# A two-layer fp32 trunk on one core: seven block products for eight in the output projections' second halves, and two hand-written orders changed

## The chip, the core and the metric

The kernel runs on one core of a Trainium2 chip. The core has a matrix engine (TensorE, PE in the profile), whose weight loads are listed apart as PEld, and four others: VectorE (DVE), ScalarE (ACT), GpSimd (POOL) and SyncE (SP). Here SP and POOL issue transfers and compute nearly nothing. The metric is device time in microseconds (us) of one execution; lower is better. A difference of about 0.2% (4.3 us here) is what a measurement of this kernel can tell from no change.

## The reference

The input is 256 tokens by 2048 features in fp32. Layer 0 is a recurrent mixer, layer 1 a windowed attention, and each ends in an output projection and is followed by a squared-ReLU MLP:

```
proj  = rms_norm(h) @ w_in                       # layer 0
lru   = rg_lru(conv(x_lru), gates) * gelu(y_lru)  # 1024 columns
hg    = hgrn2(q, f, v, g)                         # 8 heads, 1024 columns
h     = h + concat(lru, hg) @ w_out               # 2048 x 2048
h     = h + square(relu(rms_norm(h) @ w1)) @ w2   # 2048 x 8192 x 2048

q,k,v = split(rms_norm(h) @ w_qkv)                # layer 1, 16 heads of 128
o     = dilated causal attention(q, k, v)
h     = h + o @ w_o                               # 2048 x 2048
h     = h + square(relu(rms_norm(h) @ w1)) @ w2
out   = rms_norm(h)
```

The change touches `@ w_out` and `@ w_o`, the order of work in the gates of `rg_lru`, and the order in which the first block of each MLP takes its weights.

## The kernel before, in words

**Precision.** Each fp32 operand of a large product is split in two parts: `hi`, a copy rounded to the matrix engine's fp32r type, and `lo`, the rest. A product takes three matmuls: hi by hi, hi by lo, lo by hi. For a tile of weights (128 x 2048, 1 MB) ScalarE makes `hi` (line 116, "cast") and VectorE makes `lo` by a subtraction (line 117, "split").

**Weights.** The list `units` holds every tile in the order of use. `unit()` takes the next and calls `fetch()`, which loads the tile two places ahead (SP queue), casts it and splits it. Raw tiles, `hi` and `lo` have three buffers each, so the cast of a tile waits until the matmuls of the tile three places before it are done.

**Output projections.** `out_project` (line 655) runs over four column groups n of 512 columns. `tokens` (line 335) makes one group: four weight tiles (`kgs`, each with four blocks of 128 rows), two token halves j, three matmuls each: 96 matmuls of 512 columns. With `by_k` the matmuls run over the row blocks i outside and over j inside, otherwise the other way round; the first group of both projections has `by_k`. The two sums (`ps`) go into PSUM banks named `p`, three of them in turn, and `add_res` adds them to the residual `xres`. `to_features` queues the transposes to the feature layout; `turn_some` lets them run between weight tiles.

**Seven products for eight.** Both MLP products and the values of layer 1 take column groups in pairs, in `blocks` (line 663). Over half of the rows the 2x2 blocks (token halves by column groups) are multiplied with seven products instead of eight, by Winograd's form of Strassen's scheme: units `a`, `t1`, `t2`, `c`, `t3`, `d`, `t4`, 12 matmuls each. The other half of the rows is done plainly by four units `n` of 24 matmuls. The seven need sums of weight tiles (made in `combine` by a VectorE addition, line 148, and by accumulating transfers that POOL issues, into tiles `s` and `t`), sums of the left operand (`formx` or `formh`, made by `combos` and `part_forms`), and row blocks in the order `PAIRED`. `ORDERS` gives the order of the 11 units. `second` (line 780) is the pair for `@ w2`, which adds its results to `xres`.

**Order.** A planner orders the instructions of each engine by priorities (`stream` for casts, `urgent` for evictions) and by a timeline of its own. Orders by hand are added as dependencies: `mm` chains the matmuls of the large products, `after` puts one instruction behind another, `lut` keeps ScalarE's table functions together. In `lru_gates` (line 549) the weight tile fetched at that point is loaded at once, but its cast is put behind the fourth of the eight gate sigmoids (`late`, `behind`, `gates[3:4]`). The product of the last attention head, `po` (lines 932 and 933), is not in the chain, and the planner places it.

**Names.** In the traces a name is that of the tile: `p<-hi,bufb` is a large product of the left operand in `bufb` with `hi`; `po`, `pd`, `pt`, `pl` are other PSUM banks; `xall` is the residual; `z`, `q`, `gr`, `gi`, `xc` are tiles of the recurrent group.

Of the kernel before, what the change touches and what calls it, by code (L numbers as in the profile page):

```python
# [10 lines left out]
F32 = mybir.dt.float32  # L11
# [5 lines left out]
OP = mybir.AluOpType  # L17
# [3 lines left out]
P = 128  # L21
S = 256
D = 2048
KB = D // P
# [17 lines left out]
def trunk_kernel(ctx, tc, head, x, xtok, cols, tab, masks, pos, fin, w_in, w_gate, w_out, w_qkv, w_o, w1, w2, out):  # L42
# [27 lines left out]
    units = []  # L70
# [3 lines left out]
    def plan(src, n):  # L74
        units.extend((src, i) for i in range(n))

    order_of = lambda src, i: ORDERS[0 if src is w1 else 2 if src is w2 and i == 120 else 1]

    def plan2(src, i):
        for what, u in order_of(src, i):  # L80
# [4 lines left out]
    for step in ORDER.split():  # L85
        src, first, n = where[step[0]]
        units.extend((src, first(int(step[1])) + i) for i in range(n))
    units.extend((w_out, 4 * n + g) for n in range(4) for g in (2, 3, 0, 1))
    for layer in range(2):
        if layer:  # L90
            for v, heads in ((0, 24), (32, 8)):
                plan2(w_qkv, v)
                units.extend((w_qkv, v + 8 + i) for i in range(heads))
            plan(w_o, 16)
        for q in range(4):
            for src in (w1, w2):
                for n in range(0, 4, 2):
                    plan2(src, layer * 64 + q * 16 + 4 * n)
    at = [0, 0]

    class Weights:
        def __init__(self, raw, step=2048, behind=()):
# [3 lines left out]
            self.behind = list(behind)  # L106
            for at in range(0, 2048, step) if step else ():
                self.split(at, step)

        def split(self, at, n, w=None):  # L110
            h, l = self.part(at, n)
            if w is None:
                w = self.raw[:, at:at + n]
            else:
                h, l = (t.rearrange("p (k c) -> p k c", c=512) for t in (h, l))
            casts[:] = [after(A.copy(h, w), self.behind)]  # L116
            i = V.tensor_tensor(l, w, h.bitcast(F32), OP.subtract)  # L117
# [5 lines left out]
    def fetch(late=None):  # L123
        u = at[0]
        if u >= len(units):
            return
        at[0] += 1
        src, i = units[u][:2]
        with stream():
            if len(units[u]) > 2:  # L130
                combine(u, *units[u])
                return
            r = wraw.tile([P, 2048], F32, name="raw")
            loads[:] = [after(nc.sync.dma_start(r, src[i]), [])]
            if late is not None:
                late.append((u, r))
                return
            made[u] = Weights(r, 1024)

    held, waiting, read = {}, [], []  # L140
# [1 line left out]
    def combine(u, src, i, what, i0):  # L142
        def load(name, j, home=wraw):
            held[name] = home.tile([P, 2048], F32, name="raw" if home is wraw else name)
            nc.sync.dma_start(held[name], src[j])

        def add(to, x, y):
            return V.tensor_tensor(held[to], held[x], held[y], OP.add)
# [12 lines left out]
        if ahead == ("t2",):  # L161
            load("c", i0 + 5)
            nc.gpsimd.dma_start(held["t1"], src[i0 + 5], accum_op=OP.add)
            if src is w2 and i0 == LATE_SUM:
                make()
                after(add("s", "s", "c"), [made[u].ins.name])
                return
            add("s", "s", "c")
        make(2048 if what != "t2" else 0)
        if what == "t2":  # L170
            waiting.append(made[u])
        if what == "c":
            nc.gpsimd.dma_start(held["s"], src[i0 + 1], accum_op=OP.add)
# [25 lines left out]
    def unit(src, i, late=None):  # L199
        u = at[1]  # L200
        assert units[u][0] is src and units[u][1] in (None, i), (u, i)
        at[1] += 1
        if u + 2 >= at[0]:
            fetch(late)
        return made.pop(u)

    chain = []
# [1 line left out]
    def mm(*args, **kw):  # L209
        chain[:] = [after(T.matmul(*args, **kw), chain)]  # L210
# [121 lines left out]
            V.scalar_tensor_tensor(t, t, -0.5, v, op0=OP.mult, op1=OP.mult)  # L332
            V.scalar_tensor_tensor(r, t, 1.5, r, op0=OP.add, op1=OP.mult)

    def tokens(src, i0, mov, kgs=(0, 1, 2, 3), by_k=False):
        ks = range(KB)
        ps = [pmm.tile([P, 512], F32, name="p") for _ in range(2)]
        for g in kgs:
            w = unit(src, i0 + g)
            order = [(j, i) for i in range(4) for j in range(2)] if by_k else \  # L340
                [(j, i) for j in range(2) for i in range(4)]
            for j, i in order:
                k = ks[4 * g + i]
                h, l = w.part(i * 512, 512)
                xh = mov[:, k, j * P:j * P + P]
                xl = mov[:, k, S + j * P:S + j * P + P]
                first, last = g == kgs[0] and i == 0, g == kgs[-1] and i == 3
                mm(ps[j], xh, h, start=first, stop=False)
                mm(ps[j], xh, l, start=False, stop=False)
                mm(ps[j], xl, h, start=False, stop=last)  # L350
            turn_some(1)
        return ps

    def tokens_group(src, i0, rt=None, by_k=False, kgs=(0, 1, 2, 3), behind=()):
# [192 lines left out]
        split_to(bufb[:, b], xc[:, b])  # L547

    def lru_gates(gp):
        late, gates = [], []  # L550
        w = unit(w_gate, gp, late)
        gr = wk.tile([P, 4, S], F32, name="gr", bufs=1)
        gi = wk.tile([P, 4, S], F32, name="gi", bufs=1)
        for m in range(4):
            b = 4 * gp + m
            for gate, (g, bname) in enumerate(((gr, "b_a"), (gi, "b_i"))):
                p = pmm.tile([P, 512], F32, name="p")
                direct(p, w, [(gate * 8 + 2 * m + k, bufb[:, (b // 2) * 2 + k], k == 0, k == 1)
                              for k in range(2)])
# [102 lines left out]
    nrm = out_project(w_out, "nmlp0", (2, 3, 0, 1))  # L662
# [117 lines left out]
    def second(i0, n0, nrm, r2, r2n, done, gains):  # L780
        def to_x(bank, j, n, r, last):
            at = slice(n * 512, n * 512 + 512)
            with urgent():
                read[:] = [after(V.scalar_tensor_tensor(xres[:, j, at], bank, r[:, j:j + 1], xres[:, j, at],
                                                        op0=OP.mult, op1=OP.add), [])]
                if nrm and last:
                    nrm.add(j, n, 0, S if ending and (j, n) == (1, LAST) else 512)
# [19 lines left out]
        def u3(bank):  # L807
            to_x(bank, 1, n0 + 1, r2n, True)
            done(n0 + 1)

        blocks(w2, i0, n0, bufb, formh,
               {"a": lambda b: to_x(b, 0, n0, r2, False), "t1": lambda b: to_x(b, 1, n0 + 1, r2, False),
                "t2": u2, "t3": u3, **ends},
               lambda n, j, b: to_x(b, j, n0 + n, r2, (n, j) != (1, 1)))
# [2 lines left out]
    def mlp(layer, nrm, nxt, gname):  # L817
# [34 lines left out]
                second(layer * 64 + q * 16, n, ends, r2, r2n, done, gains if ends and not gname and not n else None)  # L852
        return fing

    nx1 = Norm()
    mlp(0, nrm, nx1, "nmix1")
    pairs.close()
# [71 lines left out]
    def mix(hd, st, vg, bank="po", bufs=1):  # L929
        vs = slice((hd % 8) * P, (hd % 8) * P + P)  # L930
        po = psc.tile([P, S], F32, name=bank, bufs=bufs)
        T.matmul(po, vg[:, 0, vs], st[:, :S], start=True, stop=False, skip_group_check=True)  # L932
# [6 lines left out]
    lastv = []  # L939

    def values(i0):
        v = vgs.tile([P, 2, 2, 512], F32, name="vg")
# [131 lines left out]
def _layout(a):  # L1074
# [25 lines left out]
    def gate(w):  # L1100
# [42 lines left out]
```

## Time and profile before

| | |
|---|---|
| time, median of 3 runs | 2151.3 us (2151.23 to 2152.33) |
| time of the profiled execution | 2151.35 us |
| its span, first to last instruction | 2149.5 us |
| granted clock of TensorE | 0.999 |
| HBM read | 481.76 MB, 225 GB/s over the span |
| layer 0's output projection | about 332.4 to 423.6 us of the span |
| layer 1's output projection | about 1379 to 1472.5 us of the span |

The profile page gives busy time and share of each engine, the chain of work that ended last, and groups of instructions by line. The view of waits names for each engine what ended its idle time. The view of windows gives busy time of each engine in a stretch; after the two times come the length, then PE, PEld, DVE, ACT and POOL busy with counts, the granted clock, the DMA share and GB/s. The timeline lists instructions with start and duration in us; a row that ends in x2 merges two, and brackets hold the idle time before it and its releaser.

### The profile page before, as it was taken

Reading aid. Unit: us, or ns where it says so; the run is one execution under the profiler, and the core shown is the slowest. Engines: PE = TensorE matmul, PEld = TensorE weight load, DVE = VectorE, ACT = ScalarE, POOL = GpSimd, SP = SyncE. Lnnn points to the kernel's source line nnn. Section 1 sums busy time; section 2 is a strip of 40 time slices with the busy share of each in tenths; the row PEclk is TensorE's granted clock in tenths of the full one; section 3 lists DMA queues with packets and bytes.
Section 4 is the critical chain, followed back from the end, with each engine's and each line's share of the span. In section 5 each row is a group of like instructions: output and inputs, shape, how many; then the busy total and the mean of one; then the engine's idle time right before and its main releaser. Section 6 shows DMA issues by size and latency. Waiting matters only on the chain.

```text
span 2149.5 us, 27705 instructions
## 1 busy us (share of the span) xinstructions
PE 2136.2 (99%) x11018; PEld 1830.3 (85%) x11018; DVE 1786.9 (83%) x2087; ACT 1267.6 (59%) x1407; POOL 61.8 (3%) x77
## 2 busy tenths in 40 slices
PE   9999999999999999999999999999999999999998
PEld 8999998888888888888888888888888888888887
DVE  7776787788888888889988897867988988888897
ACT  7444485566466566557665545456655755755764
POOL 0000000000000000000000000000000000000000
PEclk9999999999999999999999999999999999999999
DMA  8544445588878888887785556457878788787885
GB/s 323 175 157 157 154 149 209 179 240 268 249 240 263 257 243 243 277 245 234 240 268 198 173 160 232 157 185 226 237 240 283 240 240 260 262 241 243 272 261 156
DMA packets 68160, 485.64 MB, mean 226 GB/s; under 512 B 7600, under 2 KB 7856, under 8 KB 10048
## 3 DMA queue, kind: packets, MB, share of 16 engines
q1 hardware_dynamic: 57600, 410.89, 52.0%
q0 software_dynamic: 10144, 72.39, 18.3%
q8 instruction: 86, 1.41, 0.3%
q10 hardware_dynamic: 288, 0.61, 0.1%
q14 instruction: 42, 0.34, 0.0%
HBM read 481.76 MB, written 2.10 MB: 225 GB/s over the span
## 4 chain that ended last, share of the span: by engine, by line
PE 96%; ACT 2%; DVE 1%; DMA 0%; issue 0%; SPq 0%
PE p L210 66%; PE pd L210 13%; PE po L210 12%; PE pl L213 2%; PE pl L489 1%; PE pt L210 1%; DVE lo L117 1%; ACT hi L116 1%; DMA both_in<-in_head 0%; PE pl L911 0%; ACT gi L241 0%; ACT L241 0%; PE po L932 0%; PE pd L924 0%; ACT gr L241 0%; DVE xc L577 0%
## 5 line engine op out<-in xcount | busy, mean ns | idle before, releaser
L116 ACT CAST hi<-raw 128x2048 fp32r<-128x2048 f32 (+1 forms) x462 | 679.1, 1494 | 564.2 <-PE p L210 343.0
L117 DVE TENSOR_TENSOR lo<-raw,hi 128x2048 fp32r<-128x2048 f32 (+1 forms) x462 | 810.9, 1771 | 206.2 <-ACT hi L116 190.9
L210 PE MATMUL p<-hi,bufb 128*128 128x512 f32 x1408 | 449.0, 391 | 1.5 <-DVE z L438 1.1
L210 PE MATMUL p<-bufa,hi 128*128 128x256 f32 (+1 forms) x1792 | 367.2, 317 | 0.1
L210 PE MATMUL p<-hi,bufa 128*128 128x512 f32 x1136 | 363.3, 390 | 0.7 <-ACT bufa L271 0.7
L210 PEld LDWEIGHTS p<-hi,bufb 128*128 128x128 f32 x1408 | 264.3, 188 | 56.8 <-DVE z L438 1.5
L210 PEld LDWEIGHTS p<-bufa,hi 128*128 128x128 f32 x1792 | 294.9, 190 | 18.6 <-DVE hz L438 0.3
L210 PE MATMUL p<-lo,bufb 128*128 128x512 f32 x704 | 274.2, 390 | 0.0
L210 PE MATMUL p<-bufa,lo 128*128 128x256 f32 x1152 | 256.2, 287 | 0.0
L210 PEld LDWEIGHTS p<-hi,bufa 128*128 128x128 f32 x1136 | 213.1, 188 | 45.0 <-ACT bufa L271 0.9
L117 DVE TENSOR_TENSOR lo<-s,hi 128x2048 fp32r<-128x2048 f32 x102 | 233.1, 2285 | 14.5 <-ACT hi L116 12.3
L116 ACT CAST hi<-s 128x2048 fp32r<-128x2048 f32 x102 | 195.1, 1913 | 51.7 <-PE po L210 22.2
L210 PE MATMUL p<-lo,bufa 128*128 128x512 f32 x568 | 221.4, 390 | 0.2 <-DVE lo L117 0.2
L210 PEld LDWEIGHTS p<-bufa,lo 128*128 128x128 f32 x1152 | 189.7, 191 | 2.7
L210 PEld LDWEIGHTS p<-lo,bufb 128*128 128x128 f32 x704 | 132.2, 188 | 26.9
L210 PEld LDWEIGHTS p<-lo,bufa 128*128 128x128 f32 x568 | 106.6, 188 | 22.6 <-DVE lo L117 0.6
L210 PE MATMUL pd<-hi,bufa 128*128 128x512 f32 x288 | 95.2, 392 | 0.0
L210 PE MATMUL p<-hi,formx 128*128 128x512 f32 x288 | 94.8, 390 | 0.0
L117 DVE TENSOR_TENSOR lo<-t,hi 128x2048 fp32r<-128x2048 f32 x34 | 77.8, 2288 | 13.0 <-ACT hi L116 13.0
L210 PE MATMUL po<-hi,bufa 128*128 128x512 f32 x256 | 84.9, 393 | 0.0
L210 PE MATMUL p<-hi,formh 128*128 128x512 f32 x256 | 84.0, 389 | 0.0
L210 PE MATMUL pd<-hi,bufb 128*128 128x512 f32 x256 | 83.0, 389 | 0.0
(307 smaller groups left out, 2892.0 us busy)
## 6 DMA issues: line engine op xcount, KB each, us to landing
raw<-in_w SPq DMA_DIRECT2D x224, 1024.0 KB, 6.5
raw<-in_w_qkv SPq DMA_DIRECT2D x46, 1024.0 KB, 4.9
raw<-in_w_in SPq DMA_DIRECT2D x45, 1024.0 KB, 4.9
t<-in_w SPq DMA_DIRECT2D x32, 1024.0 KB, 6.4
t<-in_w POOLq DMA_DIRECT2D x32, 1024.0 KB, 8.9
s<-in_w POOLq DMA_DIRECT2D x32, 1024.0 KB, 9.3
raw<-in_w_out SPq DMA_DIRECT2D x16, 1024.0 KB, 4.9
raw<-in_w_o SPq DMA_DIRECT2D x16, 1024.0 KB, 4.8
```

What stands on the lines that cost most here:

```text
L116: casts[:] = [after(A.copy(h, w), self.behind)]
L117: i = V.tensor_tensor(l, w, h.bitcast(F32), OP.subtract)
L210: chain[:] = [after(T.matmul(*args, **kw), chain)]
L213: chain[:] = [after(T.transpose(out_, in_, ident), chain)]
L489: T.matmul(pl[:, j], kq[:, js], halves(qp[:, js], c, True), start=True, stop=True)
```

## The change

1. **Both output projections.** Column groups 0 and 1 go through `tokens` as before. Groups 2 and 3 go through `second`, as one pair of seven products for eight, with both multipliers 1.0 and -1.0. The weights come in the order `PAIRED`, so each `kgs` tile of the first 1024 rows holds blocks 0, 2, 4, 6 or 1, 3, 5, 7. `mixed_forms` makes the sums of the left operand out of `bufb` for each of four pairs of row blocks, at the places that `then` gives. In layer 0 the first group no longer has `by_k`.
2. **The first block of each MLP** takes its units in the order `ORDERS[1]` (n7 before n6) and no longer `ORDERS[0]`, and the first block of layer 1's MLP makes one sum of weights behind a split instead of ahead of it.
3. **The gates.** The order that put a cast behind the gate sigmoids is gone: the tile is cast where it is fetched.
4. **The last head.** Its two products are put into the matmul chain ahead of the second of the four row blocks of the last weight tile of layer 1's first column group.

```diff
-    order_of = lambda src, i: ORDERS[0 if src is w1 else 2 if src is w2 and i == 120 else 1]
+    order_of = lambda src, i: ORDERS[0 if src is w1 and i not in (0, 64, ) else 2 if src is w2 and i == 120 else 1]
...
-    units.extend((w_out, 4 * n + g) for n in range(4) for g in (2, 3, 0, 1))
+    units.extend((w_out, 4 * n + g) for n in range(2) for g in (2, 3, 0, 1))
+    plan2(w_out, 8)
...
-            plan(w_o, 16)
+            plan(w_o, 8)
+            plan2(w_o, 8)
...
-            casts[:] = [after(A.copy(h, w), self.behind)]
+            casts[:] = [after(A.copy(h, w), [])]
...
-            if src is w2 and i0 == LATE_SUM:
+            if (src is w2 and i0 == LATE_SUM) or (src is w1 and i0 == 64):
...
-    def tokens(src, i0, mov, kgs=(0, 1, 2, 3), by_k=False):
-        ks = range(KB)
+    def tokens(src, i0, mov, kgs=(0, 1, 2, 3), by_k=False, behind=(), then=()):
+        ks = PAIRED if any(src is w for w in (w_out, w_o, )) else range(KB)
...
+                if g == kgs[-1] and (i, j) == (1, 0):
+                    chain.extend(behind)
...
+            for m in then[kgs.index(g)] if then else ():
+                mixed_forms(m)
...
     def lru_gates(gp):
-        late, gates = [], []
-        w = unit(w_gate, gp, late)
+        w = unit(w_gate, gp)
...
-                    gates.append(luts["now"][-1])
-        with stream():
-            for u, r in late:
-                made[u] = Weights(r, 1024, gates[3:4])
...
-    def out_project(src, gname, kgs):
+    def mixed_forms(m):
+        z = pair.tile([P, 2, 2, P], F32, name="y1", bufs=2)
+        b = bufb[:, 2 * m:2 * m + 2].bitcast(F32)
+        V.tensor_tensor(z.rearrange("p i j c -> p i (j c)"), b[..., :S], b[..., S:], OP.add)
+        a11, a21, a12, a22 = (z[:, i, j] for i in range(2) for j in range(2))
+        combos(a22, a11, a21, a12, a11, a21, a12, a22)
+        part_forms(formh, m, 1, slice(0, 4), z.rearrange("p i j (one c) -> p one (i j) c", one=1))
+
+    def out_project(src, gname, kgs, behind=()):
         nrm = Norm()
-        for n in range(4):
-            add_res(tokens(src, 4 * n, bufb, kgs, by_k=not n), n, nrm)
+        whole = any(src is w for w in (w_out, w_o, ))
+        for n in range(2 if whole else 4):
+            then = () if not whole else ((((), (0,), (1,), (2,)), ((), (), (3,), ())) if src is w_out else
+                                         (((), (), (), (0, 1)), ((), (2,), (3,), ())))[n]
+            add_res(tokens(src, 4 * n, bufb, kgs, src is w_o and not n, () if n else behind, then), n, nrm)
             to_features(n, gname, formx if n < 2 else None)
+        if whole:
+            second(0, 2, nrm, 1.0, -1.0, lambda n: to_features(n, gname, None), None, src)
         return nrm
...
-        T.matmul(po[:, P:], vg[:, 1, vs], st[:, S:], start=False, stop=True, skip_group_check=True)
+        lastpo[:] = [after(T.matmul(po[:, P:], vg[:, 1, vs], st[:, S:], start=False, stop=True, skip_group_check=True), [])]
...
-    nrm = out_project(w_o, "nmlp1", (0, 1, 2, 3))
+    nrm = out_project(w_o, "nmlp1", (0, 1, 2, 3), lastpo)
...
-        "w_in": c(np.concatenate(w_in)), "w_gate": c(w_gate), "w_out": c(toks(n(a["rec_w_out"][0]))),
-        "w_qkv": c(np.concatenate(w_qkv)), "w_o": c(toks(n(a["attn_w_o"][0]))),
+        "w_in": c(np.concatenate(w_in)), "w_gate": c(w_gate), "w_out": c(toks(n(a["rec_w_out"][0]), PAIRED)),
+        "w_qkv": c(np.concatenate(w_qkv)), "w_o": c(toks(n(a["attn_w_o"][0]), PAIRED)),
```

In the built programs the change has these counts: PE has 24 matmuls of 512 columns fewer; VectorE has 50 instructions more; ScalarE has two fewer (32 casts of half a tile go, 22 casts of a whole tile and eight of 512 columns come); POOL issues four accumulating transfers more; SP issues as many as before.

More of the change, by code (lines that the diff above doesn't have):

```diff
@@ L101, in trunk_kernel, with __init__ @@
     class Weights:
-        def __init__(self, raw, step=2048, behind=()):
+        def __init__(self, raw, step=2048):
             self.raw = raw
@@ L105, in __init__ @@
             self.lo = wlo.tile([P, 2048], F32R, name="lo")
-            self.behind = list(behind)
             for at in range(0, 2048, step) if step else ():
@@ L121, in part, with fetch @@
             return self.hi[:, at:at + n], self.lo[:, at:at + n]
-    def fetch(late=None):
+    def fetch():
         u = at[0]
@@ L134, in fetch @@
             loads[:] = [after(nc.sync.dma_start(r, src[i]), [])]
-            if late is not None:
-                late.append((u, r))
-                return
             made[u] = Weights(r, 1024)
@@ L197, in fetch_first, with unit @@
                 made[u].split(1024 * m, 1024)
-    def unit(src, i, late=None):
+    def unit(src, i):
         u = at[1]
@@ L203, in unit @@
         if u + 2 >= at[0]:
-            fetch(late)
+            fetch()
         return made.pop(u)
@@ L653, in to_features @@
         turns.extend([-half if forms else 0, lambda half=half: work(half)] for half in range(2))
-    def out_project(src, gname, kgs):
-        nrm = Norm()
-        for n in range(4):
-            add_res(tokens(src, 4 * n, bufb, kgs, by_k=not n), n, nrm)
+    def mixed_forms(m):
[6 more added lines that the diff above has]
+    def out_project(src, gname, kgs, behind=()):
+        nrm = Norm()
+        whole = any(src is w for w in (w_out, w_o, ))
[3 more added lines that the diff above has]
+            add_res(tokens(src, 4 * n, bufb, kgs, src is w_o and not n, () if n else behind, then), n, nrm)
             to_features(n, gname, formx if n < 2 else None)
+        if whole:
+            second(0, 2, nrm, 1.0, -1.0, lambda n: to_features(n, gname, None), None, src)
         return nrm
-    nrm = out_project(w_out, "nmlp0", (2, 3, 0, 1))
     def blocks(src, i0, n0, mov, forms, events, final):
@@ L778, in first, with second @@
                                              "t3": u3}, final)
-    def second(i0, n0, nrm, r2, r2n, done, gains):
+    def second(i0, n0, nrm, r2, r2n, done, gains, src=w2):
         def to_x(bank, j, n, r, last):
@@ L783, in to_x @@
             with urgent():
-                read[:] = [after(V.scalar_tensor_tensor(xres[:, j, at], bank, r[:, j:j + 1], xres[:, j, at],
+                r = r if isinstance(r, float) else r[:, j:j + 1]
+                read[:] = [after(V.scalar_tensor_tensor(xres[:, j, at], bank, r, xres[:, j, at],
                                                         op0=OP.mult, op1=OP.add), [])]
@@ L809, in u3 @@
             done(n0 + 1)
-        blocks(w2, i0, n0, bufb, formh,
+        blocks(src, i0, n0, bufb, formh,
                {"a": lambda b: to_x(b, 0, n0, r2, False), "t1": lambda b: to_x(b, 1, n0 + 1, r2, False),
@@ L853, in mlp @@
         return fing
+    nrm = out_project(w_out, "nmlp0", (2, 3, 0, 1))
     nx1 = Norm()
@@ L937, in trunk_kernel @@
         rt = rstd(nx1)
-    lastv = []
+    lastv, lastpo = [], []
     def values(i0):
```

## The prediction

> **What bounds the kernel now.** I read the page first, then the view of waits for PE, then the chain, then windows over the stages that change.
>
> ```profile
> span 2149.5 us, 27705 instructions
> PE 2136.2 (99%) x11018; PEld 1830.3 (85%) x11018; DVE 1786.9 (83%) x2087; ACT 1267.6 (59%) x1407; POOL 61.8 (3%) x77
> ```
> ```profile
> engine line waited for: us in total, times, longest us
> PE p L210 <- DVE z L438: 1.4, 2, 1.1
> PE po L282 <- DVE e L407: 1.1, 1, 1.1
> PE p L210 <- ACT gr L241: 0.9, 1, 0.9
> PE p L210 <- ACT bufa L271: 0.7, 1, 0.7
> PE p L210 <- ACT bufb L268: 0.5, 1, 0.5
> ```
> ```profile
> 575.16 5.44 PE p L210 x24
> 580.60 5.44 PE po L210 x24
> 594.20 8.16 PE p L210 x36
> ```
> ```profile
> 334.27:430.10 95.83, 95.83 (x438) 79.52 (x439) 65.98 (x85) 53.32 (x77) 1.00 (x1) 1.00 0.60 198
> 1060.00:1093.00 33.00, 33.00 (x153) 27.41 (x153) 32.43 (x33) 23.53 (x23) 2.27 (x3) 1.00 0.81 252
> 1093.00:1136.00 43.00, 43.00 (x196) 35.69 (x195) 36.60 (x43) 26.81 (x26) 0.88 (x1) 1.00 0.78 253
> ```
>
> PE is busy for 99% of the span and waits for other engines for less than 5 us in all. The chain's two rows show a run of 24 matmuls of 512 columns followed at once by the next: 5.44 us for 24, 0.227 us each. So a matmul taken out shortens the run, as long as the other engines keep up. The first window is the projection of layer 0 with the start of its MLP: PE never idle, VectorE 66.0 of 95.8 us. The other two are the end of layer 0's MLP and the handover to layer 1, where pairs with seven products stand today beside `to_features` with forms: VectorE is busy for 98% and then 85%, and PE still has no idle time. That is the nearest precedent for the new stage.
>
> **Part 1, the matmuls.** Each projection's second half has 192 matmuls today. The pair has 7 x 12 = 84 and 4 x 24 = 96, so 180. Twice 12 are 24: -5.44 us. A reason for the gain to be smaller would be a new wait, which the next parts take up.
>
> **Part 1, the load on VectorE.**
>
> ```profile
> L117 DVE TENSOR_TENSOR lo<-raw,hi 128x2048 fp32r<-128x2048 f32 x238 | 544.9, 2289 | 133.2 <-ACT hi L116 132.7 <-ACT pT L926 0.4
> L148 DVE TENSOR_TENSOR s<-s,raw 128x2048 f32<-128x2048 f32 x34 | 77.6, 2283 | 0.0
> L612 DVE TENSOR_TENSOR formh<-y,formh 128x512 fp32r<-128x512 f32 x32 | 21.9, 684 | 0.0
> L629 DVE SCALAR_TENSOR_TENSOR xall<-p,xall 128x512 f32<-128x512 f32 x16 | 11.0, 688 | 5.1 <-PE p L210 5.1
> L615 DVE TENSOR_TENSOR y<-y 128x128 f32<-128x128 f32 x4 | 1.2, 292 | 0.1
> L117 DVE TENSOR_TENSOR lo<-raw,hi 128x1024 fp32r<-128x1024 f32 x224 | 266.0, 1221 | 73.0 <-ACT hi L116 58.2 <-PE p L210 13.2 <-ACT as L241 0.4
> 345.89 2.36 DVE L117 TENSOR_TENSOR lo<-raw,hi 128x1024 fp32r<-128x1024 f32 x2 [2.46 <-ACT hi L116]
> ```
>
> Per projection: 11 splits of whole tiles at 2.29 (25.2 us) for eight split in halves at 2.36 (18.9), so +6.3; two sums at 2.28, +4.6; four more additions to the residual at 0.69, +2.8; four `mixed_forms`, each one addition of 512 columns (0.69), four of 128 (0.29 each) and one split of a form (0.68), +10.2. Together 23.8 us. VectorE then has 66.0 + 23.8 = 89.8 us in a window of 95.8 - 2.7 = 93.1 us, 96%. Today's 30 us of idle time there are the cover, nearly used up; the precedent above ran at 98% without cost to PE. ScalarE gains, per projection, three whole casts and four short ones, about 8 us on 53.3: covered. So the load as a whole costs nothing, and the question is the order.
>
> The title "VectorE: DVE Perf Modes" of the Trainium skill, section "The DRAIN you can't avoid", says that the next VectorE operation does not start before the one in front has emptied the pipeline. By that rule the whole durations count, as I summed them, and the 96% stand. The trace differs: the two splits of 1024 merged in the last row end after 2.36 us, less than twice the 1.22 us that the row above it shows for one, so neighbours overlap by about 0.08 us and the 23.8 is an upper end.
>
> In the built order of the changed kernel VectorE's queue around the start of the pair is, in layer 0: eviction of `xall`, sum `s`, eviction, split for n7. PE needs that split 24 matmuls (5.44 us) after the last matmul of group 1, and the eviction (0.69) and split (2.29) that wait for that moment take 3.0: hidden. In layer 1 the queue is: eviction, sum, split, so 0.69 + 2.28 + 2.29 = 5.26 us against 5.44 and eight transposes: just hidden, if VectorE arrives without a backlog. But there the last two `mixed_forms`, the additions of `to_features` and two splits are queued in the 10 us before it. The bounds are 0 and one split late, 2.29; I take +0.5, nearer to the lower, since the precedent shows no wait.
>
> The four accumulating transfers more (POOL) and the 4 MB more behind them load windows whose DMA share is 0.60 today, against 0.81 in the precedent: nothing. SP issues as many loads in nearly the same order. POOL's queue holds nothing else there.
>
> **Part 1, layer 0's first group.** Without `by_k`, PE needs its second bank later.
>
> ```profile
> 332.36 0.40 PE L210 MATMUL p<-hi,bufb 128*128 128x512 f32 x1
> 332.83 0.39 PE L210 MATMUL p<-hi,bufb 128*128 128x512 f32 x1
> 334.27 0.50 PE L210 MATMUL p<-hi,bufb 128*128 128x512 f32 x1 [1.05 <-DVE z L438]
> 333.80 0.42 DVE L438 TENSOR_TENSOR z<-p,nr 128x256 f32<-128x256 f32 x1
> ```
>
> Today the fourth matmul goes to the second bank and waits until VectorE has read it (333.80 + 0.42 = 334.22). After, twelve come first: 332.36 + 12 x 0.227 = 335.08, past 334.22. The wait goes. It is 1.44 us from the third matmul to the fourth (the third starts at 332.83) for 0.23, so -1.2 us. Nothing is late behind it: `bufb` of block 6, needed sooner now, is in the third tile, 10.9 us on. Bounds 0 and -1.2.
>
> **Part 2, first block of the MLP.** The pair finishes column group 3 early (after `t3`) and group 2 last. Unit n7 reads group 3, n6 group 2, so n7 first is the order that the pair needs: n6 now comes 72 matmuls (16.3 us) after the pair. The handover 1093 to 1136 has that order today with PE at 43.00 of 43.00. Zero; with n6 first, the transposes and splits of group 2 would have to fit into 5.4 us.
>
> **Part 3, the gates.**
>
> ```profile
> 268.22 0.40 PE L210 MATMUL p<-bufb,hi 128*128 128x256 f32 x2
> 269.39 0.46 ACT L241 ACTIVATE gr<-p,c__88 128x256 f32<-128x256 f32 x1
> 272.55 1.99 ACT L116 CAST hi<-raw 128x1024 fp32r<-128x1024 f32 x2
> 302.60 0.42 ACT L241 ACTIVATE q<-q 128x256 f32<-128x256 f32 x1 [0.20 <-DVE q L585]
> 303.56 0.50 PE L210 MATMUL p<-bufb,hi 128*128 128x256 f32 x2 [0.36 <-DVE z L438]
> 305.88 1.99 ACT L116 CAST hi<-raw 128x1024 fp32r<-128x1024 f32 x2
> 308.30 0.50 PE L210 MATMUL p<-bufb,hi 128*128 128x256 f32 x2 [0.89 <-ACT gr L241]
> ```
>
> In both groups the built order now has the cast ahead of the first sigmoid `gr` instead of behind the fourth. The cast takes 1.99 us, and every sigmoid is queued behind it; the matmuls of the fourth product wait for the first sigmoid, as only three banks `p` exist. In the first group PE has no wait today; the cast can start when PE begins the gates (268.2), so `gr` moves from 269.4 to about 271, and the fourth product, due at about 271, waits some 0.4 us. In the second the cast moves from 305.9 to behind `q` at 302.6, so `gr` ends at about 305.6 where the fourth product was due at 304.3: the old waits (0.36 and 0.89) go and 1.3 to 1.5 come. Together +0.5 us; bounds -1.6 (all waits gone) and +2.5 (one cast more in front of PE, and the transposes behind it).
>
> **Part 4, the last head.**
>
> ```profile
> 1397.79 2.00 ACT L116 CAST hi<-raw 128x1024 fp32r<-128x1024 f32 x2 [0.26 <-PE p L210]
> 1398.87 2.36 DVE L117 TENSOR_TENSOR lo<-raw,hi 128x1024 fp32r<-128x1024 f32 x2 [2.18 <-ACT hi L116]
> 1401.66 0.59 PE L932 MATMUL po<-pT,vg 128*128 128x256 f32 x2
> 1402.93 0.50 PE L210 MATMUL p<-hi,bufb 128*128 128x512 f32 x1 [0.46 <-ACT bufb L268]
> ```
>
> Today `po` runs at 1401.66 and PE waits 0.46 for its cast to `bufb`. Moved twelve matmuls (2.7 us) ahead, `po` is done before ScalarE leaves the cast at 1399.8, and `bufb`'s `hi` is there by 1400.2. Its `lo` stands on VectorE behind the split (to 1401.2) and two additions of 512 columns (1.4), so at about 1403.0, a few tenths late for the third matmul. I take -0.4; bounds -0.7 and +0.5.
>
> **The sum.** -5.4 - 1.2 + 0.5 + 0.5 - 0.4 = -6.0 us. The profiled execution took 2151.35 (its span and 1.85 around it), the same as the median of 2151.3. So 2145.3 us. Lower end: -5.4 - 1.2 - 1.6 - 0.7 = -8.9, 2142.4. Upper end of the likeliest case: +2.5 gates and +2.3 late split, by_k and last head without gain, -0.6, 2150.7.
>
> **The rivals.**
> (a) VectorE becomes the bound in the pairs, and the kernel is slower. Place: the 11 units of each pair, mostly layer 1's. Each time that a split comes a whole split late PE loses 2.29. Without the +0.5 the sum is 2144.8; two late splits give 2149.4, three 2151.7, just over today's time, and five 2156.3. For it: 96% load, and forms put between splits. Against: the window at 98% without idle PE. Decides from three late splits on.
> (b) The gain is mostly paid back: gates at +2.5, one split late, by_k's 1.2 gained, the last head's wait unchanged: -5.4 - 1.2 + 2.5 + 2.3 = -1.8, 2149.5. For it: strictly ordered queues on ScalarE and VectorE with more in front of what PE waits for.
> (c) PE isn't what binds, so that 24 matmuls fewer save nothing: only the by_k and last-head waits would move, 2149.7. For it: PEld is busy for just 85%. Against: the back-to-back rows, and windows where nothing else is full. The Trainium skill, "Perfetto Trace Analysis", section "Identifying the Most-Contended Engine", holds matmul busy time to be a bad measure of the distance to the roofline and counts weight loads instead; by that, PE would have 15% left. The 0.227 us between matmuls is steady, so I give it little.
> (d) The change does what it says and new waits don't appear: all gate waits go too, and the time is 2142.4.
>
> **How the numbers follow.** Forecast 2145.3 (2143.5 to 2147.0): 0.52. (d): 0.13. (b): 0.20. (c): 0.04. (a): 0.11. Range 2142.4 to 2150.5, which leaves out (a) and little else. Faster by over 0.2% (under 2147.0; 0.2%, 4.3 us, is about what a measurement of this kernel tells from no change): 0.65. Within 0.2%: 0.24, (b) and (c). Slower: 0.11.
>
> **What would show it.** The runs of 24 and 36 matmuls in the pairs at 5.44 and 8.16 us without idle time; no wait of PE for L438 at the projection's start; a wait of PE for `gr` in both gate groups of under 1.5 us each; PE's wait for `lo` at n7 in layer 1 under 1 us. I am wrong if PE waits for line 117 several times in a pair, or if the gates cost more than 2 us.

## The result and the profile after

The changed kernel takes 2143.5 us (median of six runs, 2142.8 to 2144.7) where the kernel before takes 2151.3 (six runs): a ratio of 0.9964, with a 95% interval of 0.9951 to 0.9976. The profiled execution took 2143.43 us with a span of 2141.7, against 2149.5 before: 7.8 us less, where 6.0 had been forecast.

Most lines of code have moved by one to ten: matmul L210 is now L208, the cast L116 is L117, the split L117 is L118, the sigmoids L241 are L239, `z<-p` L438 is L440, the split of an operand L268 is L266 and its `lo` L267.

The page of the changed kernel, span and busy time:

```profile
span 2141.7 us, 27727 instructions
PE 2130.3 (99%) x10994; PEld 1825.7 (85%) x10994; DVE 1824.1 (85%) x2137; ACT 1281.4 (60%) x1405; POOL 65.3 (3%) x81
```

PE's waits in the changed kernel, all that the view lists:

```profile
engine line waited for: us in total, times, longest us
PE po L280 <- DVE e L409: 1.1, 1, 1.1
PE p L208 <- ACT bufa L269: 0.8, 1, 0.8
PE p L208 <- ACT gr L239: 0.7, 1, 0.7
PE p L208 <- DVE z L440: 0.3, 1, 0.3
```

PE lost 5.9 us of busy time and is still at 99%. The first two waits lie at the start of the span, as before. The wait of 1.05 us at the projection's start and the 0.46 behind the last head are gone; those in the gates are 0.27 and 0.72 instead of 0.36 and 0.89; and no wait for a split (L118) has come.

The chain through the new pair of layer 0, then through the handover from its last units to n7 in layer 1 (start, duration):

```profile
376.90 2.72 PE po L208 x12
379.62 2.72 PE p L208 x12
382.34 0.44 PE pl L211 x4
382.77 5.48 PE p L208 x24
388.25 0.44 PE pl L211 x4
388.69 2.75 PE po L208 x12
391.44 8.16 PE p L208 x36
...
1422.53 2.72 PE po L208 x12
1425.25 2.72 PE p L208 x12
1427.98 0.44 PE pl L211 x4
```

Every row starts where the last one ends, in units of 12 matmuls at 2.72 us. PE has no idle time in either pair, although VectorE is nearly full. The window of the changed kernel that matches the prediction's first one, from the fourth matmul of layer 0's projection to the first of its MLP; after the window come its length, then PE, PEld, DVE, ACT, POOL, the clock, the DMA share and GB/s:

```profile
332.94:425.88 92.94, 92.94 (x427) 77.17 (x426) 85.19 (x108) 59.91 (x76) 2.72 (x3) 1.00 0.73 228
```

VectorE is busy for 85.2 of 92.9 us, 92%, up from 66.0 of 95.8. How near that is to costing something, the split of n7 in layer 1 shows, the last row here (VectorE's timeline of the changed kernel, and the chain's row of the matmuls that want it):

```profile
1422.86 0.69 DVE L626 SCALAR_TENSOR_TENSOR xall<-p,xall 128x512 f32<-128x512 f32 x1
1423.46 2.29 DVE L146 TENSOR_TENSOR s<-s,raw 128x2048 f32<-128x2048 f32 x1
1425.66 2.29 DVE L118 TENSOR_TENSOR lo<-raw,hi 128x2048 fp32r<-128x2048 f32 x1
```
```profile
1428.41 2.75 PE p L208 x12
```

The split ends at 1427.95, 0.46 us before PE starts n7. In layer 0 it ends at 381.93 for 382.77, 0.84 us ahead.

With PE's matmuls numbered in both traces and set against each other, start by start, the 7.8 us are: -5.4 in the two pairs, from 24 matmuls fewer; -1.35 at the start of layer 0's projection; -0.6 behind the last head; -0.45 in the gates; -0.25 behind the last matmul; and +0.3 in the first 20 us of the span. No edit is aimed at those 20 us; by their end the kernels below lie up to 1.4 us apart, and from there to the gates they keep step within 0.02 us. So a small effect is read between two matmuls of the same trace, and not from the whole time. For the gates these are the first matmul of the gates and the first of the projection:

```profile
268.55 0.40 PE L208 MATMUL p<-bufb,hi 128*128 128x256 f32 x2
332.25 0.40 PE L208 MATMUL p<-hi,bufb 128*128 128x512 f32 x1
```

From one to the other are 63.70 us; in the kernel before it was 332.36 - 268.22 = 64.14.

### The profile page after: what moved, and what is told of

Read it like the earlier page. It is cut to its first block, busy times and chain, and to the rows that moved or that the text cites. A ratio compares the mean times of both kernels' runs of the same rounds, so it can differ in the third digit from the quotient of the medians.

```text
span 2141.7 us, 27727 instructions
## 1 busy us (share of the span) xinstructions
PE 2130.3 (99%) x10994; PEld 1825.7 (85%) x10994; DVE 1824.1 (85%) x2137; ACT 1281.4 (60%) x1405; POOL 65.3 (3%) x81
## 4 chain that ended last, share of the span: by engine, by line
PE 97%; DVE 1%; ACT 1%; DMA 0%; issue 0%; SPq 0%
PE p L208 65%; PE po L208 14%; PE pd L208 13%; PE pl L211 2%; PE pl L491 1%; PE pt L208 1%; DVE lo L118 0%; ACT hi L117 0%; DMA both_in<-in_head 0%; PE pl L922 0%; PE po L943 0%; PE pd L935 0%; PE pd L475 0%; PE pl L921 0%; ACT bufa L269 0%; PE po L944 0%
## 5 line engine op out<-in xcount | busy, mean ns | idle before, releaser
L117 ACT CAST hi<-raw 128x2048 fp32r<-128x2048 f32 (+1 forms) x444 | 673.9, 1539 | 563.5 <-PE p L208 335.3
L118 DVE TENSOR_TENSOR lo<-raw,hi 128x2048 fp32r<-128x2048 f32 (+1 forms) x444 | 805.8, 1828 | 174.5 <-ACT hi L117 158.6
L208 PE MATMUL p<-hi,bufb 128*128 128x512 f32 x1264 | 404.8, 391 | 0.0
L208 PE MATMUL p<-bufa,hi 128*128 128x256 f32 (+1 forms) x1792 | 367.3, 317 | 0.1
L208 PE MATMUL p<-hi,bufa 128*128 128x512 f32 x1136 | 363.4, 390 | 0.8 <-ACT bufa L269 0.8
L208 PEld LDWEIGHTS p<-bufa,hi 128*128 128x128 f32 x1792 | 294.7, 190 | 18.6 <-DVE hz L440 0.3
L208 PEld LDWEIGHTS p<-hi,bufb 128*128 128x128 f32 x1264 | 237.2, 188 | 49.3 <-DVE bufb L267 0.3
L208 PE MATMUL p<-bufa,lo 128*128 128x256 f32 x1152 | 256.2, 287 | 0.0
L118 DVE TENSOR_TENSOR lo<-s,hi 128x2048 fp32r<-128x2048 f32 x108 | 246.8, 2285 | 9.6 <-ACT hi L117 7.4
L208 PEld LDWEIGHTS p<-hi,bufa 128*128 128x128 f32 x1136 | 213.1, 188 | 45.2 <-ACT bufa L269 1.1
L208 PE MATMUL p<-lo,bufb 128*128 128x512 f32 x632 | 246.2, 389 | 0.0
L117 ACT CAST hi<-s 128x2048 fp32r<-128x2048 f32 x108 | 206.6, 1913 | 47.6 <-PE po L208 22.4
L208 PE MATMUL p<-lo,bufa 128*128 128x512 f32 x568 | 221.6, 390 | 0.1
L208 PEld LDWEIGHTS p<-bufa,lo 128*128 128x128 f32 x1152 | 189.7, 191 | 2.7
L208 PEld LDWEIGHTS p<-lo,bufb 128*128 128x128 f32 x632 | 118.7, 188 | 24.2
L208 PEld LDWEIGHTS p<-lo,bufa 128*128 128x128 f32 x568 | 106.7, 188 | 22.8 <-DVE lo L118 0.8
L208 PE MATMUL po<-hi,bufb 128*128 128x512 f32 (+1 forms) x320 | 102.4, 386 | 0.0
L208 PE MATMUL pd<-hi,bufa 128*128 128x512 f32 x288 | 95.2, 392 | 0.0
L208 PE MATMUL p<-hi,formx 128*128 128x512 f32 x288 | 94.8, 390 | 0.0
L208 PE MATMUL p<-hi,formh 128*128 128x512 f32 x288 | 94.5, 389 | 0.0
L118 DVE TENSOR_TENSOR lo<-t,hi 128x2048 fp32r<-128x2048 f32 x36 | 82.4, 2289 | 13.0 <-ACT hi L117 13.0
L208 PE MATMUL po<-hi,bufa 128*128 128x512 f32 x256 | 84.9, 393 | 0.0
```

What stands on the lines that cost most here:

```text
L117: casts[:] = [after(A.copy(h, w), [])]
```

## The experiments

The theory to test: PE sets the time, each matmul of 512 columns is worth 0.227 us, and VectorE, nearly full, stays just ahead of it. Unless a text says otherwise, each kernel is the changed kernel with one edit, and is compared with 2143.5. Single runs of these kernels are good to about 1 us (the changed kernel's own six spread over 1.9), so where less is in question the waits and the starts of matmuls in the trace decide.

**Layer 1's projection without the pair.** Here layer 0 alone has the pair. It is the test of whether PE binds.

```diff
-            plan(w_o, 8)
-            plan2(w_o, 8)
+            plan(w_o, 16)
...
-        whole = any(src is w for w in (w_out, w_o, ))
+        whole = src is w_out
```

> The changed kernel, but layer 1's output projection runs its second pair of column groups plainly again (eight products, no forms, the MLP's first block with n6 first as before), so it has twelve matmuls of 512 columns more. Theory: PE binds and each matmul costs its 0.227 us, so +2.7 us: span 2144.4, time 2146.2. Rival (c), PE isn't what binds: no difference, or less time because VectorE has 23 us less work.

Measured: 2146.2 us (ten runs, 2145.8 to 2146.5), a ratio of 0.9975 to the kernel before (0.9966 to 0.9985). Twelve matmuls cost 2.7 us, which is 12 x 0.227; by the traces, layer 1's pair is 2.72 us longer from start to start. Rival (c), that PE isn't what binds, falls, though PEld stands at 85% in both kernels.

**Layer 0's first group with `by_k` again.** Why did the wait at the projection's start go?

```diff
-            add_res(tokens(src, 4 * n, bufb, kgs, src is w_o and not n, () if n else behind, then), n, nrm)
+            add_res(tokens(src, 4 * n, bufb, kgs, not n, () if n else behind, then), n, nrm)
```

> The changed kernel, but layer 0's first column group runs with by_k again. My theory: the wait for the second bank had gone because twelve matmuls now come before the first that needs it; with by_k the fourth matmul needs it, so PE waits again about 1.05 us for line 440, and the span grows from 2141.7 by about 1.2 to 2142.9 us. Rival: the wait had gone because VectorE's queue ahead of it changed with the gates; then no wait comes back, and the span stays within 0.2 us.

Measured: 2143.2, and no wait is listed there. The third and fourth matmul take 0.79 us together where the changed kernel has 0.62, and the stretch loses 0.2 us in all instead of 1.2:

```profile
332.25 0.79 PE L208 MATMUL p<-hi,bufb 128*128 128x512 f32 x2
```

So the reason given in the prediction, that twelve matmuls come first without `by_k`, is not needed in this kernel.

**The cast behind the fourth sigmoid again,** in both gate groups (`fetch` hands the raw tile back, and the tile is cast with the old dependency):

```diff
-        w = unit(w_gate, gp)
+        late, gates = [], []
+        w = unit(w_gate, gp, late)
...
+                    gates.append(luts["now"][-1])
+        with stream():
+            for u, r in late:
+                made[u] = Weights(r, 1024, gates[3:4])
```

> The changed kernel, but the cast stands behind the fourth gate sigmoid again, as before. Theory from the prediction: removing the order cost 0.5 us, so PE's waits in the gates shrink and the span falls to 2141.2. Rival, read from the trace after: PE's waits in the second gate group were 0.36 and 0.89 us with the order and are 0.27 and 0.72 without it, and the first group has none in either; then the old waits come back and the span grows by 0.1 to 0.3 us. A third: the order moved other work as well, and the span moves by over 1 us.

Measured: 2143.4. PE's waits in the gates are those of the kernel before, 0.9 and 0.4, in place of 0.7 and 0.3, and no wait came at the projection's start either. The same two matmuls as above, in this run:

```profile
268.02 0.40 PE L212 MATMUL p<-bufb,hi 128*128 128x256 f32 x2
332.16 0.40 PE L212 MATMUL p<-hi,bufb 128*128 128x512 f32 x1
```

They are 64.14 us apart, as in the kernel before. So removing the order saves 0.44 us; the time doesn't show it, since this trace's first 20 us are 0.5 us shorter than the changed kernel's. By parts, the changed kernel loses 0.2 in the first gate group, and gains 0.27 in the second and 0.36 between the two, at 284 to 294 us. There no wait is listed in either trace and the planner's order of small matmuls differs; why that stretch is shorter is not shown.

**Both of these undone.** The two traces suggested that each edit hides what the other one does.

> Layer 0's first projection group runs its blocks in turn again (by_k), and the cast of a group's second weights stands behind the fourth sigmoid of the gates again; each of these alone left the time where it was. Theory, from the traces of those two: the second bank of the projection's first group comes free when VectorE's queue reaches L440's z<-p, at 332.4 to 332.9 us without the gates' order and at 334.0 with it, and TensorE wants that bank at 332.3 with by_k and about 335 without. Either edit alone is then enough, and only both together bring the wait of before back: 1.0 to 1.3 us of TensorE idle for z at 332 us, beside 0.4 for z and 0.9 for the sigmoid in the gates; about 2144.7. Rival: something else of the change (the planner's other costs, the seven products) moved L440 ahead; then no wait at 332 us and 2143.4.

Measured: 2144.8, and the wait is back. PE's waits with both undone:

```profile
PE p L212 <- DVE z L444: 1.4, 2, 1.1
```

VectorE's read of the bank that PE wants next (timelines: with `by_k` alone, with the old gate order alone, with both):

```profile
332.07 0.42 DVE L440 TENSOR_TENSOR z<-p,nr 128x256 f32<-128x256 f32 x1
```
```profile
333.60 0.42 DVE L444 TENSOR_TENSOR z<-p,nr 128x256 f32<-128x256 f32 x1
```
```profile
333.63 0.42 DVE L444 TENSOR_TENSOR z<-p,nr 128x256 f32<-128x256 f32 x1
```

Without the old gate order VectorE reaches this read 1.5 us earlier and ends it at 332.49, just as the fourth matmul is due with `by_k` (the third starts at 332.25, one takes 0.23). With the old order the read ends at 334.0, and only the absence of `by_k` helps: there PE wants the bank twelve matmuls after 332.16, at 334.9. The two undone together cost 1.3 us from start to start; the old gate order alone costs nothing at this place, `by_k` alone 0.2. Either edit alone is enough for most of the gain.

**The gates, a third way:** the second group's cast behind the second sigmoid, the first group as in the changed kernel.

```diff
+                if late and len(gates) == 2:
+                    with stream():
+                        for u, r in late:
+                            made[u] = Weights(r, 1024, gates[-1:])
```

> The changed kernel, but in the second gate group the cast stands behind the second gate sigmoid. Theory: PE's wait of 0.72 us for the first sigmoid goes, as two banks are free before the cast takes ScalarE, and the wait of 0.27 us for line 440 stays: span 2141.0. Rival: the wait moves to the third sigmoid behind the cast and stays as long: span within 0.2 us of 2141.7.

Measured: 2144.1; one wait for `gr` of 1.5 us in place of 0.7. Neither text has this size: the wait did move to the third sigmoid, as the rival says, but it doubled, and the second group loses 0.95 us from start to start. The place in the queue decides which sigmoid is late, and by how much.

**The last head's products left to the planner.**

```diff
-    nrm = out_project(w_o, "nmlp1", (0, 1, 2, 3), lastpo)
+    nrm = out_project(w_o, "nmlp1", (0, 1, 2, 3))
```

> The changed kernel, but the last head's two products are not in the matmul chain; the planner puts them twelve matmuls later, as before. Theory: PE waits again about 0.46 us for the cast of line 266 into bufb, 0.67 us with the lost pace, and the span grows to 2142.4. Rival: the wait went because the split order in front of it changed; then no wait comes, and the span stays within 0.2 us.

Measured: 2144.4, 0.8 us more, and 1.4 from start to start at this place. PE's waits that came:

```profile
PE p L208 <- DVE bufb L267: 0.5, 1, 0.5
PE p L208 <- ACT bufb L266: 0.5, 1, 0.5
```

Both parts of `bufb` are late without the move, `lo` too: VectorE does the pair's two additions `y<-bufb` (1397.85 to 1399.14) in front of it there. With the move neither is listed as late, but `lo` is just in time. The changed kernel's rows, VectorE's and PE's:

```profile
1398.13 0.42 DVE L267 TENSOR_TENSOR bufb<-po,bufb 128x256 fp32r<-128x256 f32 x1
```
```profile
1398.61 0.73 PE L208 MATMUL p<-hi,bufb 128*128 128x512 f32 x2
```

`lo` ends at 1398.55, 0.06 us before the first matmul that reads it. In the kernel before only `hi` was late, and there the same place cost 0.6 us.

**The first blocks of the MLPs with n6 before n7.**

```diff
-    order_of = lambda src, i: ORDERS[0 if src is w1 and i not in (0, 64, ) else 2 if src is w2 and i == 120 else 1]
+    order_of = lambda src, i: ORDERS[0 if src is w1 else 2 if src is w2 and i == 120 else 1]
```

> The changed kernel, but the first block of each MLP takes unit n6 before n7 again, with PE's instructions in the same places. Theory: the transposes of column group 2 end just where n6 would start, and ScalarE's and VectorE's copies of them (four of about 0.4 us on each) lie between, so PE waits 1 to 4 us at each of the two blocks: span 2143.7 to 2149.7. Rival: the copies are done in time, or the planner's order covers them: no wait, the span within 0.3 us.

Measured: 2158.7, 15 us more, where 2 to 8 had been expected. PE's waits, and three windows at the first of the two places:

```profile
PE p L208 <- ACT bufa L269: 5.0, 3, 2.7
PE p L208 <- DVE bufa L270: 4.8, 3, 2.4
```
```profile
425.26:428.67 3.41, 0.88 (x4) 0.30 (x2) 3.41 (x4) 2.12 (x3) 0.85 (x1) 1.00 0.67 274
428.67:435.50 6.83, 5.32 (x12) 4.09 (x13) 2.93 (x8) 0.86 (x2) 0.00 (x0) 0.50 0.90 186
435.50:437.00 1.50, 1.50 (x8) 1.21 (x7) 0.00 (x0) 0.00 (x0) 0.00 (x0) 1.00 0.98 388
```

The mechanism is the one that was named (group 2's features aren't ready); the price has two parts. The late matmuls lose 10.2 us from start to start, over both layers. The other 5 us are the clock: while PE waits it falls to 0.50, and the matmuls behind the wait start 0.43 us apart instead of 0.23, for 5.3 us in layer 0 and 4.8 in layer 1.

**How much room VectorE has.** First, splits done twice; the result stays the same. In two units of each pair (t1 and n7), then in all 11:

```diff
-            i = V.tensor_tensor(l, w, h.bitcast(F32), OP.subtract)
+            for _ in range(2 if self.twice else 1):
+                i = V.tensor_tensor(l, w, h.bitcast(F32), OP.subtract)
```

> The changed kernel, with VectorE's splits for units t1 and n7 done twice in both projections' pairs, 4.6 us more work per pair ahead of the point where the margin is thinnest (the split for n7 ends 0.8 us in layer 0 and 0.5 us in layer 1 before PE starts n7). Theory of the thin margin: PE waits; the planner now puts the sum s behind that split, which gives 2.3 us back, so 1.3 to 1.8 us in each pair, span 2144.3 to 2145.3. Rival, capacity alone counts: the window of the projection has 7.7 us of idle VectorE time, so 4.6 more cost nothing, span within 0.3 us.

> The changed kernel, with all eleven splits of both pairs done twice: 25 us more on VectorE per pair, whose pair stage has 44.8 us of work in 48.1 today. Rival (a) of the prediction asks where VectorE becomes the bound. Theory: beyond the idle time of the pair and of the units prefetched ahead PE pays for all of it, 17 to 22 us per projection, span 2176 to 2186. Rival: the neighbouring blocks take up most of it, and the span grows by under 20 us in all.

Measured: 2156.8 (13 us more, several times the theory) and 2180.7 (37 us more, within its range, which proves little beside the other's miss). That miss left open whether VectorE has no room at all or something else was late, so n7's split alone was repeated, whole and by half:

> Only n7's split, the last one before a pair's second products, is done twice in both layers (2.29 us of VectorE more in each pair, the result unchanged). Theory: in the changed kernel this split ends 0.46 us (layer 1) and 0.8 to 0.9 us (layer 0) before TensorE asks for it, and what is over that margin falls on TensorE in full: waits of about 1.8 and 1.4 us, 3.2 in all, if the clock stays at 1.00: about 2146.7. If a wait of this length already lowers the granted clock as the waits of 4.3 us did in the run with two splits doubled (0.5 for 3 to 5 us behind them), 1.6 to 2.5 us more each: up to 2151. Rival: the loss there came from the other doubled split (t1) or from the queue's order, and VectorE has more room than 0.5 us: no wait over 0.5 us, under 2144.5.

> The first half of n7's split is done twice in both layers (1.2 us of VectorE more in each pair, the result unchanged). Theory of the margin: waits of about 0.75 us in layer 1 and 0.3 to 0.4 in layer 0, the clock stays at 1.00: about 2144.6. Rival (more room than the split's end shows): no wait, 2143.4. Other rival (any wait of TensorE lowers the clock): 2147 or more.

Measured: 2159.1 and 2154.5, 16 and 11 us more; the theory had 3.2 and 1.1. VectorE's timeline of the run with half the split repeated shows why:

```profile
379.05 2.28 DVE L119 TENSOR_TENSOR lo<-raw,hi 128x2048 fp32r<-128x2048 f32 x1
381.25 0.68 DVE L798 SCALAR_TENSOR_TENSOR xall<-po,xall 128x512 f32<-128x512 f32 x1
381.85 0.68 DVE L798 SCALAR_TENSOR_TENSOR xall<-p,xall 128x512 f32<-128x512 f32 x1
382.45 2.28 DVE L119 TENSOR_TENSOR lo<-s,hi 128x2048 fp32r<-128x2048 f32 x1
384.65 1.22 DVE L121 TENSOR_TENSOR lo<-raw,hi 128x1024 fp32r<-128x1024 f32 x1
```

The planner put the repeat (L121) behind two sums into x (L798) and the next split. PE waits for the repeat, so this dose also measured the 3.4 us of other work in front of it. What is clean is the difference of the two runs: 1.06 us more of VectorE gave 1.06 us more from start to start in layer 0 (4.82 against 3.76) and 1.07 in layer 1 (5.81 against 4.74). Past this operand's margin, VectorE's time falls on PE in full. So a last kernel did the half split once beforehand and the whole one after it:

```diff
+            if self.twice:
+                V.tensor_tensor(l[:, :1024], w[:, :1024], h[:, :1024].bitcast(F32), OP.subtract)
             i = V.tensor_tensor(l, w, h.bitcast(F32), OP.subtract)
```

> The first half of n7's split is done once beforehand and then the whole split (the result unchanged). In the two runs before, the repeat was put by the planner behind two sums into x and another split, so that the lower part came 3.5 us later than the repeat itself takes; here the built order keeps the whole split right behind one sum into x in layer 0 and behind that and a formx difference in layer 1. Theory of the margin (0.46 us in layer 1, 0.87 in layer 0, then one to one): VectorE's part is later by 1.14 + 0.60 us in layer 0 and 1.14 + 1.20 in layer 1, so TensorE waits 0.85 and 1.9 us for lo; 2146.2 with the clock at 1.00 throughout, or up to 2148.6 if the longer wait lowers it for a few us. Rival (VectorE is late for another reason than its place in the queue, and the splits of n7 have no margin at all or a large one): waits of 1.7 and 2.3 us and more, or none.

Measured: 2146.1. PE's timeline, the two matmuls that wait:

```profile
383.41 0.50 PE L212 MATMUL p<-lo,bufb 128*128 128x512 f32 x1 [0.70 <-DVE lo L121]
1430.98 0.50 PE L212 MATMUL p<-lo,bufb 128*128 128x512 f32 x1 [1.69 <-DVE lo L121]
```

From start to start that is 0.96 and 1.94 us lost, for 0.85 and 1.9 expected from the margins. So the margins read off the timeline are right to about 0.1 us. The clock after these waits, and after the longer one in the run with the half split repeated behind (windows of the two kernels):

```profile
1428.00:1432.00 4.00, 2.31 (x12) 1.70 (x11) 4.00 (x5) 3.66 (x5) 0.00 (x0) 1.00 0.06 10
1432.00:1436.00 4.00, 4.00 (x19) 3.27 (x18) 4.00 (x3) 0.00 (x0) 0.86 (x1) 1.00 0.90 274
```
```profile
385.92 0.50 PE L212 MATMUL p<-lo,bufb 128*128 128x512 f32 x1 [3.51 <-DVE lo L121]
```
```profile
383.05:386.46 3.41, 0.54 (x2) 0.48 (x3) 3.41 (x3) 2.03 (x4) 0.86 (x1) 1.00 0.00 0
386.46:389.87 3.41, 3.41 (x9) 2.65 (x8) 3.27 (x6) 0.00 (x0) 0.00 (x0) 0.50 0.94 166
```

After 1.69 us of waiting the clock stays at 1.00. After 3.51 it is half for 3.41 us, from 386.46 on, half a microsecond after the matmuls have begun again.

No kernel here beats the changed one by more than a single run can tell; the nearest is the one with `by_k` again, 2143.2, and its trace loses 0.2 us against the changed kernel's at the projection's start.

## Why the prediction was right, and where not

The forecast of 2145.3 was 1.8 us too high; the direction, the main mechanism and the range were right. Of the 1.8 us, the gates are 0.95, n7's split 0.5, and the projection's start and the last head some 0.15 each. Step by step:

- **24 matmuls fewer, -5.4.** Right. The pairs run at 2.72 us for 12 matmuls without idle time, and taking one pair back costs 2.7 us.
- **VectorE's load, 96%, at no cost.** Right, and the load was summed too high: 85.2 of 92.9 us, 92%, for 89.8 of 93.1. The durations added up to 22.9 us more, near the 23.8; but 3.7 of them overlap with a neighbour, which the prediction had named as the reason to call 23.8 an upper end. Rival (a) did not come: no wait for a split is listed. But the 92% hide how near it was: n7's margin in layer 1 is 0.46 us, and each microsecond past it counts in full.
- **n7's split in layer 1, +0.5.** It cost nothing, so the +0.5 was mis-sized. The backlog is small: VectorE comes from other work without a pause and starts the eviction at 1422.86, 0.33 us after PE leaves group 1 (1422.53). Eviction, sum and split then take 5.09 us for the 5.26 summed, and PE has 5.44 us of matmuls and four transposes (0.44) to do first, so 0.46 us are left.
- **Layer 0's first group, -1.2.** The size was about right (1.35). "After, twelve come first" would have been reason enough with VectorE's queue as it was before: the run with the old gate order shows that. In the changed kernel it is not needed. With `by_k` back the wait stays away but for 0.2 us, because VectorE's queue has the read of the bank 1.5 us earlier once the gates' order is gone; both undone bring a wait of 1.1 us back. The step looked at PE's order and kept VectorE's queue as it was, though another part of the same change reorders it.
- **The gates, +0.5.** Wrong in sign: -0.45 from start to start, in the kernel before and in both runs with the old order. In the first group the cast runs ahead of `gr` (268.63 and 271.04 in the fence below), as foreseen, and PE's wait is not there, only 0.2 us of pace. In the second, `gr` ends at 305.26 for the forecast "about 305.6", and the fourth product was due at 304.59 for 304.3, behind a wait of 0.27 for z that had been taken as gone; so the wait is 0.72 for "1.3 to 1.5", and the group gains 0.27. The other 0.36 lie between the groups, where the forecast did not look and no run gives the cause.
- **The last head, -0.4.** Mis-sized: -0.6, near its lower bound of -0.7. `lo` is not "a few tenths late": with the products early, VectorE has it done 0.06 us before PE asks for it. Left to the planner, both `hi` and `lo` are late by 0.5, so in the changed kernel the move is worth 1.4.
- **n7 first in the MLPs' first blocks, 0.** Right, and worth far more than it seemed: the reverse order costs 15 us.

ScalarE's timeline of the changed kernel, the gates of both groups:

```profile
268.63 2.00 ACT L117 CAST hi<-raw 128x1024 fp32r<-128x1024 f32 x2 [1.25 <-PE p L208]
271.04 0.45 ACT L239 ACTIVATE gr<-p,c__88 128x256 f32<-128x256 f32 x1
...
302.60 1.98 ACT L117 CAST hi<-raw 128x1024 fp32r<-128x1024 f32 x2
304.80 0.46 ACT L239 ACTIVATE gr<-p,c__88 128x256 f32<-128x256 f32 x1
```

Rival (c) falls with the layer-1 run. Rival (b) falls with the traces: neither the 2.5 us of the gates nor the late split came. Rival (d) came half true: no new waits, but the gate waits stayed, a little shorter.

## What to carry to other kernels

Where the matrix engine is busy all the time, price a matmul at its start-to-start pace and look at how long before its use each late operand is ready: that margin, not the busy share, says how much more work the other engine can take in front of that operand. Before giving one edit the credit for a wait that goes, read the queue of the engine that ends the wait in the new order, since another edit may have moved it. A repeated instruction is a clean dose only where the built order keeps it next to the original. Where the start of the span varies by more than the effect, compare two matmuls within a trace, and not the whole time.

## What was not expected of the hardware

A wait of PE costs more than itself once it is long. After waits of 0.70 and 1.69 us the granted clock stayed at 1.00. After one of 3.51 us it was 0.50 for 3.41 us, and after 1.67 and 2.37 us with two matmuls between them (the run with n6 first, layer 0) for 6.83 us; in such a stretch the matmuls start 0.43 us apart. The 3.41 us in front of the fall need not be empty: PE was busy for 0.54 of them in the first case and for 0.88 in the second, by the windows above. In the run with n7's split repeated whole the two waits took 10.6 us from start to start, and the two pairs became 14.9 us longer, the rest being the slow clock. The Trainium skill, "TensorE: Matmul & The Clock Gate", Part 1, gives two states, half rate after an idle window of about 3.4 us and full rate after as long a busy one, with windows that run freely; the 0.50, the 1.00 and the 3.41 and 6.83 us (one window and two) of the slow stretches agree, and so does a fall that comes after the wait's end. Where between 1.7 and 3.5 us of unbroken idle time the fall begins was not measured.
